# Seven block products in place of eight for the second MLP product, with weight sums on GpSimd and weight chunks prepared two ahead

## The chip, the cores and the metric

The kernel runs on one core of a Trainium2 chip. A core has five engines with a queue each: TensorE (PE, with its weight loads shown as PEld), VectorE (DVE), ScalarE (ACT), GpSimd (POOL) and SyncE (SP, which issues the DMAs here). The metric is the device time of one execution in microseconds; the kernel before takes 947.76 us, the median of three runs (947.66 to 948.29).

## The reference

Two decoder layers on 256 tokens of width 1024, all in float32. Each layer runs three token mixers side by side, gates and sums them, and then a squared-ReLU MLP. Only the MLP's last line is computed in another way by the change:

```python
def hybrid_layer(x, ...):
    hn = rms_norm(x, norm1_g)
    proj = hn @ w_in                       # 1024 -> 8216 columns, three mixers, gates
    ...
    x = x + mixed @ w_out
    h2 = rms_norm(x, norm2_g)
    x = x + jnp.square(jax.nn.relu(h2 @ w_ff1)) @ w_ff2      # 1024 -> 4096 -> 1024
    return x
```

## The kernel before

Every product with weights is a float32 product in three terms. A number is split into a rounded part (`hi`, in the type fp32r) and a rest (`lo`); TensorE adds hi x hi, hi x lo and lo x hi into one PSUM bank. Weights come from memory in chunks of 1 MB (128 partitions x 2048 numbers). `prepare` (L148) loads a chunk into one of three `raw` buffers and `split` (L133) makes its `hi` on ScalarE (L138, two casts of 128x1024) and its `lo` on VectorE (L139, two subtractions of 128x1024), into three buffers each. A table, `ORDER` (L142), lists the chunks in the order of use, and `chunk` (L161) prepares `AHEAD` = 1 chunk beyond the one asked for. A scheduler then places the instructions on the engines' queues; each engine works its queue in order.

The MLP of a layer is the stage that is changed. `ff1(p)` (L758), p = 0 to 15, makes 256 of the 4096 hidden columns: 48 matmuls with 256 moving columns from chunk 42 + p, then the ReLU on VectorE straight from PSUM (L764), the square on ScalarE (L765), and the split of the result, `fh` (L766 on ScalarE, L767 on VectorE). `ff2(p)` (L769) multiplies these 256 hidden columns with 256 rows of the second weight matrix (chunk 58 + p): 2 halves of 128 hidden columns x 2 halves of 128 tokens x 2 halves of 512 outputs x 3 terms = 24 matmuls with 512 moving columns, added up in four banks `acc` that live through the stage (8 block products of three matmuls for each p). The loop runs `ff2(p)`, `ff1(p + 3)`, `ff2(p + 1)` and so on, so that the hidden columns are three steps ahead. The last four p come from chunks 70 to 73, cut by output half, so that the first half of the output can be finished earlier. The end of a layer is one VectorE instruction for each of the four banks (L804): times `r2`, the inverse mean square, plus `x`; then the next layer's norm, or the store of the output.

Buffers of 128x1024 numbers come from a ring of 14 (`s4`, function `slab`), of 128x512 numbers from a ring of 4 (`s2`, `half`): a new tile takes the oldest place and waits until all readers of that place are done.

Of the kernel before, what the change touches and what calls it, by code (L numbers as in the profile page):

```python
# [18 lines left out]
P = 128  # L19
# [24 lines left out]
def kernel(ctx: ExitStack, tc: tile.TileContext, xT, xtok, gbias, wbig, wsml, aup, cst, prm, out):  # L44
# [223 lines left out]
    for l in range(DEPTH):  # L268
# [500 lines left out]
        def ff2(p):  # L769
            h = hs.pop(p)  # L770
            w = [z.rearrange("p (k c) -> p k c", c=D) for z in chunk(l, 58 + p)]
            for k in range(2):
                for t in range(2):
                    ts = slice(t * P, (t + 1) * P)
                    for n in range(2):
                        rows_mm(acc[t][n], w, k, slice(512 * n, 512 * n + 512), h[:, 0, k, ts], h[:, 1, k, ts],
                                p == 0 and k == 0, False)

        NT = 4
        ff1(0)  # L780
        ff1(1)
        acc = [[Bank(pmx, f"fa{l}{t}{n}", [P, 512]) for n in range(2)] for t in range(2)]
        ff1(2)
        for p in range(16 - NT):
            ff2(p)
# [7 lines left out]
        for n in range(2):
            for a in range(2):
                w = [z.rearrange("p (k c) -> p k c", c=512) for z in chunk(l, 70 + 2 * n + a)]
                for t in range(2):
                    ts = slice(t * P, (t + 1) * P)
                    for k in range(4):
                        h = hs[16 - NT + 2 * a + k // 2]
                        rows_mm(acc[t][n], w, k, slice(0, 512), h[:, 0, k % 2, ts], h[:, 1, k % 2, ts],  # L800
                                False, a == 1 and k == 3)
                    if a == 1:
                        xs = x[:, t, 512 * n:512 * n + 512]
                        nc.vector.scalar_tensor_tensor(xs, acc[t][n].t, r2[:, t:t + 1], xs, op0=OP.mult, op1=OP.add)  # L804
                        if l + 1 < DEPTH:
                            norm.squares(t, n)
                        else:
                            nc.sync.dma_start(out[:, t, 512 * n:512 * n + 512], xs)
# [43 lines left out]
def _pack(w_in, brs, w_out, w1, w2):  # L852
    c = []
    cut = lambda a, n: w_in[:, a:a + n]
    c += _tok(cut(GV, 512)) + _tok(cut(GG, 512)) + _chan(cut(GQ, 512)) + _chan(cut(GK, 512))
# [4 lines left out]
    for w in brs:  # L860
        for h in range(2):
            c.append(w[:, 512 * h:512 * h + 512].reshape(4, P, 512).transpose(1, 0, 2).reshape(P, CHW))
    left, right = _tok(w_out[:, :512]), _tok(w_out[:, 512:])
    c += [left[0], right[0], left[1], right[1]]
    c += _chan(w1)
    for p in range(12):
        c.append(w2[T * p:T * (p + 1)].reshape(2, P, D).transpose(1, 0, 2).reshape(P, CHW))
    c += _tok(w2[12 * T:, :512]) + _tok(w2[12 * T:, 512:])
    return c


# [55 lines left out]
```

## Time and profile before

| | before |
|---|---|
| median of three runs | 947.76 us |
| the profiled execution | 946.03 us |
| its span in the trace | 944.3 us |
| mean granted TensorE clock (1 is 2.4 GHz) | 0.995 |
| PE busy | 918.5 us, 97%, 5188 matmuls |
| DVE busy | 624.0 us, 66% |
| ACT busy | 454.0 us, 48% |
| POOL busy | 65.9 us, 7%, 84 instructions |

The durations in the prediction come from the one profiled execution (946.03 us, 1.7 us below the median of the runs). A row with a line and an engine gives busy time and the mean of one; a timeline row gives start, duration, engine, line and operation. An instruction's duration includes the time in which it stands started and blocked, so the spacing of two neighbours in a full queue tells more than their durations.

### The profile page before, as it was taken

To read this page: it belongs to the slowest core of one execution; us is meant where nothing else is said; L and a number is where in the kernel's file an instruction comes from. 1 tells how busy PE (TensorE), PEld (TensorE's weight loads), DVE (VectorE), ACT (ScalarE), POOL (GpSimd) and SP (SyncE) were. 2 spreads that over 40 slices of the span, in tenths; PEclk is the share of its full clock that TensorE was granted. 3 is DMA by queue.
4 is the path that set the end of the run, shared out by engine and by line. 5 is a ranking of instruction groups with operands and counts; after the bars stand their busy time and mean duration, and the time that the engine had idled before them with its cause. 6 is when DMAs were issued, how large, how long until landed. Compare 5 with 4: busy or idle time off the path is not lost.

```text
span 944.3 us, 12865 instructions
## 1 busy us (share of the span) xinstructions
PE 918.5 (97%) x5188; PEld 789.2 (84%) x5188; DVE 624.0 (66%) x984; ACT 454.0 (48%) x647; POOL 65.9 (7%) x84
## 2 busy tenths in 40 slices
PE   7799999999999999999999999999999999999998
PEld 5578888788788999999887788878887899999996
DVE  5995668477876655555669955765788675555553
ACT  5756444454435544444557553435443454444441
POOL 1551000000110000000002300000002000000000
PEclk9799999999999999999999999999999999999999
DMA  9547343544455555555442554344544545545541
GB/s 333 219 159 262 141 145 110 190 170 154 170 178 178 179 179 189 199 192 179 178 173 106 197 216 145 134 145 178 188 147 166 185 160 203 179 178 185 194 157 45
DMA packets 26203, 164.91 MB, mean 175 GB/s; under 512 B 3040, under 2 KB 3296, under 8 KB 7328
## 3 DMA queue, kind: packets, MB, share of 16 engines
q1 hardware_dynamic: 26144, 164.10, 48.7%
q8 instruction: 40, 0.66, 0.3%
q14 instruction: 19, 0.16, 0.0%
HBM read 163.04 MB, written 1.05 MB: 174 GB/s over the span
## 4 chain that ended last, share of the span: by engine, by line
PE 85%; DVE 10%; issue 2%; ACT 1%; DMA 1%; SPq 0%; POOL 0%; DVEq 0%
PE fa L75 19%; PE bg L75 10%; PE wo L75 5%; DVE lo L139 4%; PE br L75 3%; PE gk L75 3%; PE gq L75 2%; PE lq L75 2%; PE lo L75 2%; PE gg L75 2%; PE lv L75 2%; PE mv L75 2%; PE gv L75 2%; PE mk L75 2%; PE sc L75 1%
## 5 line engine op out<-in xcount | busy, mean ns | idle before, releaser
L138 ACT CAST hi<-raw 128x1024 fp32r<-128x1024 f32 x296 | 301.4, 1047 | 384.9 <-issue 112.0
L139 DVE TENSOR_TENSOR lo<-raw,hi 128x1024 fp32r<-128x1024 f32 x296 | 362.5, 1244 | 139.4 <-ACT hi L138 139.0
L75 PE MATMUL fa<-hi,fh 128*128 128x512 f32 x512 | 162.3, 390 | 0.0
L75 PEld LDWEIGHTS fa<-hi,fh 128*128 128x128 f32 x512 | 96.2, 188 | 19.6
L75 PE MATMUL fa<-lo,fh 128*128 128x512 f32 x256 | 100.0, 391 | 0.0
L75 PE MATMUL bg<-hi,xha 128*128 128x512 f32 x192 | 77.3, 404 | 4.1 <-ACT hi L138 4.1
L75 PE MATMUL bg<-lo,xha 128*128 128x512 f32 x192 | 76.2, 397 | 5.0 <-DVE lo L139 5.0
L75 PE MATMUL bg<-hi,xla 128*128 128x512 f32 x192 | 75.8, 395 | 0.0
L75 PEld LDWEIGHTS fa<-lo,fh 128*128 128x128 f32 x256 | 48.2, 188 | 8.9
L75 PEld LDWEIGHTS bg<-lo,xha 128*128 128x128 f32 x192 | 36.7, 191 | 13.7 <-DVE lo L139 6.5
L75 PEld LDWEIGHTS bg<-hi,xha 128*128 128x128 f32 x192 | 36.6, 191 | 13.0 <-ACT hi L138 4.3
L75 PEld LDWEIGHTS bg<-hi,xla 128*128 128x128 f32 x192 | 36.6, 191 | 7.7
L75 PE MATMUL wo<-hi,mh 128*128 128x512 f32 x64 | 25.7, 401 | 0.0
L75 PE MATMUL wo<-hi,ml 128*128 128x512 f32 x64 | 25.0, 390 | 0.0
L75 PE MATMUL wo<-lo,mh 128*128 128x512 f32 x64 | 25.0, 390 | 0.0
L414 DVE SCALAR_TENSOR_TENSOR gate<-bg,ny,gb 128x512 f32<-128x512 f32 x24 | 17.3, 748 | 9.2 <-PE bg L75 9.2
L767 DVE TENSOR_TENSOR fh<-fs,fh 128x512 fp32r<-128x512 f32 x32 | 21.9, 684 | 0.0
L721 DVE SCALAR_TENSOR_TENSOR gate<-gate,br 128x512 f32<-128x512 f32 x24 | 16.4, 682 | 6.3 <-PE br L75 6.2
L765 ACT ACTIVATE fs<-fs 128x512 f32<-128x512 f32 x32 | 20.1, 628 | 0.1
L766 ACT CAST fh<-fs 128x512 fp32r<-128x512 f32 x32 | 19.7, 616 | 0.0
L75 PE MATMUL lq<-xha,hi 128*128 128x256 f32 x64 | 18.6, 291 | 0.0
L75 PE MATMUL gk<-xha,hi 128*128 128x256 f32 x64 | 18.5, 289 | 0.0
(542 smaller groups left out, 2201.0 us busy)
## 6 DMA issues: line engine op xcount, KB each, us to landing
raw<-in_wbig_dram SPq DMA_DIRECT2D x147, 1024.0 KB, 4.7
gb<-in_gbias_dram SPq DMA_DIRECT2D x12, 256.0 KB, 3.2
xT<-in_xT_dram SPq DMA_DIRECT2D x4, 256.0 KB, 4.8
raw<-in_wbig_dram SPq DMA_DIRECT2D x4, 256.0 KB, 6.1
x<-in_xtok_dram SPq DMA_DIRECT2D x2, 512.0 KB, 8.7
out_dram<-x SPq DMA_DIRECT2D x4, 256.0 KB, 2.0
cs<-in_cst_dram SPq DMA_DIRECT2D x1, 752.0 KB, 10.4
raws<-in_wsml_dram SPq DMA_DIRECT2D x2, 256.0 KB, 4.3
```

The costliest lines, as they stand in the source:

```text
L75: self._chain(nc.tensor.matmul(o, lhsT=lhsT, rhs=rhs, start=start, stop=stop, skip_group_check=True))
L138: nc.scalar.copy(hi[:, sl], raw[:, sl])
L139: nc.vector.tensor_sub(lo[:, sl], raw[:, sl], hi[:, sl])
L414: nc.vector.scalar_tensor_tensor(g[:, t], bs[t].t, r[:, t:t + 1], bias, op0=OP.mult, op1=OP.add)
L721: nc.vector.scalar_tensor_tensor(g[:, t], g[:, t], 1.0, b.t, op0=OP.add, op1=OP.mult)
L765: nc.scalar.activation(s, s, AF.Square)
L766: nc.scalar.copy(h[:, 0], s)
L767: nc.vector.tensor_sub(h[:, 1], s, h[:, 0])
```

## The change

The second MLP product is computed in Strassen's form (Winograd's variant). Tokens, hidden columns and outputs are each cut into two halves (128 tokens, 16 x 128 hidden columns, 512 outputs). In place of eight block products of the halves there are seven, each between a sum or difference of hidden blocks and a sum or difference of weight blocks, each in a PSUM bank of its own (four of the pool `pmx`, three of `pmm`).

- The weight chunk p now holds four 512-column blocks: two hidden halves x two output halves. `sums` makes three sums from them on GpSimd before the split: `t` (128x1024), one block written over a block of `raw` (128x512), and `t4` (128x512). Besides `hi` and `lo` of the chunk it makes the split of `t` (`th`, `tl`) and of `t4` (`t4h`, `t4l`).
- `ff1(p)` puts the ReLU on ScalarE, makes three sums of hidden blocks on VectorE (128x256, 128x128, 128x128) and splits eight blocks (128x1024) in place of four.
- `ff2` makes 7 x 3 = 21 matmuls of 512 columns for each p in place of 24.
- At the end of a layer the seven banks are combined with seven VectorE or ScalarE instructions and four that add to `x`. p = 14 and 15 of all seven products come last.
- `AHEAD` is 2 for all chunks of the kernel, the ring `s2` has 9 places, and the space that is set aside for DMA descriptors is smaller. The weights of both MLP products are laid out in another order in memory.

```diff
-AHEAD = 1
+AHEAD = 2
-    s2 = ctx.enter_context(tc.tile_pool(name="s2", bufs=4))
+    s2 = ctx.enter_context(tc.tile_pool(name="s2", bufs=9))
+    def sums(tag, raw):
+        b = raw.rearrange("p (i c) -> p i c", c=512)
+        t, t4 = slab(f"t{tag}", shape=(P, 2, 512)), half(f"t4{tag}")
+        nc.gpsimd.tensor_add(t, b[:, 0:4:3], b[:, 1:2].to_broadcast([P, 2, 512]))
+        nc.gpsimd.tensor_add(b[:, 1], t[:, 0], b[:, 3])
+        nc.gpsimd.tensor_add(t4, b[:, 1], b[:, 2])
+        hi, lo = split(tag, raw, CHW)
+        th, tl = slab(f"th{tag}", F32R, (P, 2, 512)), slab(f"tl{tag}", F32R, (P, 2, 512))
+        t4h, t4l = half(f"t4h{tag}", F32R), half(f"t4l{tag}", F32R)
+        for r, h, o in ((t, th, tl), (t4, t4h, t4l)):
+            nc.scalar.copy(h, r)
+            nc.vector.tensor_sub(o, r, h)
...
-    ORDER += [42, 43, 44] + [j for p in range(13) for j in (58 + p, 45 + p)][:-2] + [57, 70, 71, 72, 73]
+    ORDER += [42, 43, 44] + [j for p in range(13) for j in (58 + p, 45 + p)] + [71, 72, 73]
...
-        ready[l, j] = split(f"{l}_{j}", raw, CHW)
+        ready[l, j] = sums(f"{l}_{j}", raw) if j >= 58 else split(f"{l}_{j}", raw, CHW)
...
+        SIDES = {"P1": (0, "11"), "Q6": (6, "T2"), "P7": (4, "T3"), "Q4": (3, "T4"), "P2": (2, "21"), "P5": (5, "T1"),
+                 "P3": (7, "22")}
...
-            nc.vector.tensor_scalar(s, b.t, 0.0, None, op0=OP.max)
-            nc.scalar.activation(s, s, AF.Square)
-            nc.scalar.copy(h[:, 0], s)
-            nc.vector.tensor_sub(h[:, 1], s, h[:, 0])
+            nc.scalar.activation(s, b.t, AF.Relu)
+            nc.scalar.activation(q[:, 0:4], s, AF.Square)
+            nc.vector.tensor_sub(q[:, 4:6], q[:, 0:4:3], q[:, 1:2].to_broadcast([P, 2, P]))
+            nc.vector.tensor_add(q[:, 6], q[:, 0], q[:, 5])
+            nc.vector.tensor_sub(q[:, 7], q[:, 6], q[:, 2])
+            h = hs[p] = [slab(f"fh{p}", F32R, shape=(P, 8, P)), slab(f"fl{p}", F32R, shape=(P, 8, P))]
+            nc.scalar.copy(h[0], q)
+            nc.vector.tensor_sub(h[1], q, h[0])
+        def ff2(name, p, w):
+            i, side = SIDES[name]
+            b, (hh, hl), (wh, wl) = acc[name], hs[p], w
+            b.mm(b.t, hh[:, i], wh[side], p == 0, False)
+            b.mm(b.t, hh[:, i], wl[side], False, False)
+            b.mm(b.t, hl[:, i], wh[side], False, p == 15)
...
+        for p in range(14):
+            w = chunk(l, 58 + p)
+            for name in SIDES:
+                ff2(name, p, w)
             if p + 3 < 16:
                 ff1(p + 3)
...
+        for name in SIDES:
+            for p in (14, 15):
+                ff2(name, p, w[p - 14])
+            z = acc[name].t
+            if name == "P1":
+                nc.scalar.copy(p1, z)
...
+            else:
+                nc.vector.tensor_add(cv_, z, cv_)
+                put(0, 1, cv_, nr2)
```

In the changed program the order of the queues is as follows at three places of the first layer. VectorE, one step of the MLP loop of before (chunk 50 is for `ff1(8)`, chunk 64 for `ff2(6)`; `fs` and `fh` belong to `ff1`):

```order
L139 TENSOR_TENSOR lo_50_3194<-raw_50_3191,hi_50_3193 128x1024 x2
L764 TENSOR_SCALAR fs_3186<-f_7__3136 128x512
L139 TENSOR_TENSOR lo_64_3226<-raw_64_3223,hi_64_3225 128x1024 x2
L767 TENSOR_TENSOR fh_3185<-fs_3186,fh_3185 128x512
L139 TENSOR_TENSOR lo_51_3289<-raw_51_3286,hi_51_3288 128x1024 x2
```

The same step now (`fq` and `fl` belong to `ff1(7)`, `tl` and `t4l` to the sums of chunk 64):

```order
L139 TENSOR_TENSOR lo_50_3240<-raw_50_3237,hi_50_3239 128x1024 x2
L139 TENSOR_TENSOR lo_64_3313<-raw_64_3305,hi_64_3312 128x1024
L787 TENSOR_TENSOR fq_3295<-fq_3295 128x256
L788 TENSOR_TENSOR fq_3295<-fq_3295 128x128
L789 TENSOR_TENSOR fq_3295<-fq_3295 128x128
L792 TENSOR_TENSOR fl_3302<-fq_3295,fh_3301 128x1024
L155 TENSOR_TENSOR tl_64_3319<-t_64_3307,th_64_3318 128x1024
L139 TENSOR_TENSOR lo_64_3313<-raw_64_3305,hi_64_3312 128x1024
L155 TENSOR_TENSOR t4l_64_3321<-t_64_3308,t4h_64_3320 128x512
L139 TENSOR_TENSOR lo_51_3350<-raw_51_3347,hi_51_3349 128x1024 x2
```

A step of VectorE grows from six instructions, of which five have both inputs in SBUF, to eleven, all with both inputs in SBUF. The half of chunk 64 that holds the rewritten block is split after `tl`, as the last but one of the step.

GpSimd, from the last work of the first layer's mixers on, of before:

```order
L610 TENSOR_SCALAR ly<-ly 128x4
L723 TENSOR_TENSOR gate_1181<-gate_1181,gate_422 128x512 x2
L723 TENSOR_TENSOR gate_1580<-gate_1580,gate_616 128x512 x2
L322 TENSOR_SCALAR hr<-ny 128x2
L352 TENSOR_TENSOR mkro<-mku,tabs_4185 128x512
```

Two steps of the MLP loop now, in which `t` first waits for VectorE and for TensorE, the readers of the ring place that it takes:

```order
L147 TENSOR_TENSOR t_63_3197<-raw_63_3195 128x1024 [waits DMAHW7_49,DVE_49,PE_49]
L148 TENSOR_TENSOR raw_63_3195<-t_63_3197,raw_63_3195 128x512 [waits DMAHW4_49,DVE_49,Pool_49]
L149 TENSOR_TENSOR t_63_3198<-raw_63_3195 128x512 [waits Pool_49]
L147 TENSOR_TENSOR t_64_3307<-raw_64_3305 128x1024 [waits DMAHW1_49,DVE_49,PE_49]
L148 TENSOR_TENSOR raw_64_3305<-t_64_3307,raw_64_3305 128x512 [waits DMAHW6_49,DVE_49,Pool_49]
L149 TENSOR_TENSOR t_64_3308<-raw_64_3305 128x512 [waits Pool_49]
```

GpSimd had nothing between the mixers and the next layer (`gate`, then `hr`); now 16 x 3 sums stand there for each layer.

TensorE, the end of the first layer's MLP now, from the first use of the rewritten half of the last chunk's `lo` on (`fa0P`, `fa0Q` are banks of the seven products):

```order
L75 MATMUL fa0P_2748<-lo_73_4206,fh_4194 128x512
L75 MATMUL fa0P_2748<-hi_73_4205,fl_4195 128x512
L75 MATMUL fa0Q_2749<-lo_73_4206,fh_4194 128x512
L75 MATMUL fa0Q_2749<-hi_73_4205,fl_4195 128x512
L75 MATMUL fa0Q_2751<-t4l_73_4214,fh_4194 128x512
L75 MATMUL fa0Q_2751<-t4h_73_4213,fl_4195 128x512
L75 MATMUL fa0P_2754<-hi_72_4124,fh_4071 128x512
L75 MATMUL fa0P_2754<-lo_72_4125,fh_4071 128x512
L75 MATMUL fa0P_2754<-hi_72_4124,fl_4072 128x512
L75 MATMUL fa0P_2754<-hi_73_4205,fh_4194 128x512
L75 MATMUL fa0P_2754<-lo_73_4206,fh_4194 128x512
L75 MATMUL fa0P_2754<-hi_73_4205,fl_4195 128x512
```

Of before, the last six matmuls stood at the same place in one bank:

```order
L75 MATMUL fa_2652<-hi_73_4012,fh_3913 128x512
L75 MATMUL fa_2652<-lo_73_4013,fh_3913 128x512
L75 MATMUL fa_2652<-hi_73_4012,fh_3913 128x512 x2
L75 MATMUL fa_2652<-lo_73_4013,fh_3913 128x512
L75 MATMUL fa_2652<-hi_73_4012,fh_3913 128x512
```

The matmuls of the last two chunks are mixed now, so that twelve are left when the last halves are split.

## Rows read from the trace of the kernel before

**Rows 1.** The profile page, busy time (us), share of the span, instructions.
```profile
PE 918.5 (97%) x5188; PEld 789.2 (84%) x5188; DVE 624.0 (66%) x984; ACT 454.0 (48%) x647; POOL 65.9 (7%) x84
```

**Rows 2.** Chain of waits, first layer's MLP: start us, us, engine, tile, line, instructions.
```profile
299.16 3.00 PE f__2526 L75 x25
...
343.62 5.75 PE f__2946 L75 x48
349.37 5.47 PE fa L75 x24
...
468.86 10.01 PE fa L75 x44
```

**Rows 3.** Windows: one loop step; both MLP stages. Busy us and (instructions) per engine, clock.
```profile
338.15:349.37 11.22, 11.22 (x74) 10.26 (x73) 6.11 (x6) 5.04 (x7) 0.00 (x0) 1.00 0.55 191
...
299.20:478.90 179.70, 179.70 (x1157) 164.13 (x1155) 102.00 (x110) 84.17 (x111) 0.00 (x0) 1.00 0.50 178
761.70:940.50 178.80, 178.76 (x1147) 163.15 (x1145) 96.82 (x102) 77.57 (x97) 0.00 (x0) 1.00 0.46 165
```

**Rows 4.** Groups of VectorE and ScalarE in 315.7 to 450.3 us: busy us, mean ns.
```profile
L139 DVE TENSOR_TENSOR lo<-raw,hi 128x1024 fp32r<-128x1024 f32 x48 | 57.8, 1224 | 33.6 <-ACT hi L138 33.6
...
L138 ACT CAST hi<-raw 128x1024 fp32r<-128x1024 f32 x49 | 50.1, 1046 | 76.8 <-PE fa L75 30.5 <-PE f__2851 L75 3.6 <-PE f__3326 L75 3.6
```

**Rows 5.** Timeline of GpSimd, 57 to 73 us: start us, us, operation.
```profile
57.23 3.22 POOL L438 TENSOR_TENSOR az<-az,rTa 128x1024 f32<-128x1024 f32 x1 [14.36 <-ACT az L436]
...
67.27 1.39 POOL L329 TENSOR_TENSOR tabs<-cs,prm 128x64 f32<-128x64 f32 x1
...
72.67 0.32 POOL L329 TENSOR_TENSOR tabs<-cs,prm 128x64 f32<-128x64 f32 x1
```

**Rows 6.** Timeline of VectorE, 56.9 to 67.2 us.
```profile
56.97 1.22 DVE L139 TENSOR_TENSOR lo<-raw,hi 128x1024 fp32r<-128x1024 f32 x1
58.10 2.90 DVE L352 TENSOR_TENSOR mqro<-mqu,tabs 128x512 f32<-128x512 f32 x1
...
66.44 0.68 DVE L358 TENSOR_TENSOR mqro<-mqro,mqtmp 128x512 f32<-128x512 f32 x1
67.05 0.29 DVE L174 SCALAR_TENSOR_TENSOR mqt<-mqy 128x16 f32<-128x16 f32 x1
```

**Rows 7.** Timeline of VectorE and GpSimd, 247 to 252 us.
```profile
247.56 1.13 DVE L614 SCALAR_TENSOR_TENSOR ymls<-nu,ly,lo 128x128 f32<-128x128 f32 x4
...
247.62 1.27 POOL L723 TENSOR_TENSOR gate<-gate,gate 128x512 f32<-128x512 f32 x1
250.04 1.29 POOL L723 TENSOR_TENSOR gate<-gate,gate 128x512 f32<-128x512 f32 x1 [1.14 <-DVE gate L721]
...
250.40 2.01 DVE L139 TENSOR_TENSOR lo<-raw,hi 128x1024 fp32r<-128x1024 f32 x1 [0.44 <-ACT hi L138]
```

**Rows 8.** TensorE after waits: timeline rows, with the idle time before in brackets.
```profile
27.61 0.79 PE L75 MATMUL bg<-hi,xha 128*128 128x512 f32 x1 [4.09 <-ACT hi L138]
...
35.21 0.63 PE L75 MATMUL bg<-hi,xla 128*128 128x512 f32 x1
35.64 0.63 PE L75 MATMUL bg<-hi,xha 128*128 128x512 f32 x1
...
498.58 0.74 PE L75 MATMUL z<-gs,us 96*128 96x256 f32 x4 [2.00 <-DVE gs L379]
```

**Rows 9.** Windows around those waits; the column before the last two is the granted clock.
```profile
33.00:35.00 2.00, 2.00 (x8) 1.71 (x7) 2.00 (x9) 0.24 (x1) 0.00 (x0) 0.50 0.51 147
...
497.00:499.00 2.00, 0.42 (x3) 0.42 (x4) 1.94 (x3) 1.85 (x3) 2.00 (x4) 1.00 0.25 95
```

**Rows 10.** Waits of TensorE for weights: us in total, times, longest us.
```profile
PE bg L75 <- DVE lo L139: 5.0, 3, 2.8
PE bg L75 <- ACT hi L138: 4.1, 1, 4.1
```

**Rows 11.** Timeline of VectorE at the end of the program.
```profile
940.50 0.75 DVE L804 SCALAR_TENSOR_TENSOR x<-fa,nr,x 128x512 f32<-128x512 f32 x1 [1.97 <-PE fa L75]
```

More of the change, by code (lines that the diff above doesn't have):

```diff
@@ L140, in split @@
         return hi, lo
+    def sums(tag, raw):
[10 more added lines that the diff above has]
+            nc.vector.tensor_sub(o, r, h)
+        hi, lo = (a.rearrange("p (i c) -> p i c", c=512) for a in (hi, lo))
+        side = lambda m, u, u4: {"11": m[:, 0], "T2": m[:, 1], "21": m[:, 2], "22": m[:, 3], "T1": u[:, 0],
+                                 "T3": u[:, 1], "T4": u4}
+        return side(hi, th, t4h), side(lo, tl, t4l)
     ORDER = ["s", 10, 11, 20, 21, 8, 9, 22, 23, 12, 13, 0, 1, 4, 5, 6, 7, 24, 25, 14, 15, 16, 17, 26, 27, 2, 3, 18, 19]
     ORDER += [28, 29, 30, 31, 32, 34, 36, 33, 35, 37, 38, 39, 40, 41]
-    ORDER += [42, 43, 44] + [j for p in range(13) for j in (58 + p, 45 + p)][:-2] + [57, 70, 71, 72, 73]
+    ORDER += [42, 43, 44] + [j for p in range(13) for j in (58 + p, 45 + p)] + [71, 72, 73]
     ORDER = [(l, j) for l in range(DEPTH) for j in ORDER]
@@ L755 @@
         hs = {}
-        acc = []
+        acc = {}
+        SIDES = {"P1": (0, "11"), "Q6": (6, "T2"), "P7": (4, "T3"), "Q4": (3, "T4"), "P2": (2, "21"), "P5": (5, "T1"),
+                 "P3": (7, "22")}
         def ff1(p):
@@ L761, in ff1 @@
                 norm.inverse()
-            h = hs[p] = slab(f"fh{p}", F32R, shape=(P, 2, 2, T))
-            s = half(f"fs{p}", shape=(P, 2, T))
-            nc.vector.tensor_scalar(s, b.t, 0.0, None, op0=OP.max)
-            nc.scalar.activation(s, s, AF.Square)
-            nc.scalar.copy(h[:, 0], s)
-            nc.vector.tensor_sub(h[:, 1], s, h[:, 0])
[L769 to L785, printed above, removed]
+            s = half(f"fs{p}", shape=(P, 4, P))
+            q = slab(f"fq{p}", shape=(P, 8, P))
+            nc.scalar.activation(s, b.t, AF.Relu)
+            nc.scalar.activation(q[:, 0:4], s, AF.Square)
+            nc.vector.tensor_sub(q[:, 4:6], q[:, 0:4:3], q[:, 1:2].to_broadcast([P, 2, P]))
@@ L786 @@
+        for p in range(3):
+            ff1(p)
+        for i, name in enumerate(SIDES):
+            acc[name] = Bank(pmx if i < 4 else pmm, f"fa{l}{name}", [P, 512])
+        for p in range(14):
+            w = chunk(l, 58 + p)
+            for name in SIDES:
+                ff2(name, p, w)
             if p + 3 < 16:
                 ff1(p + 3)
-        for p in range(16 - NT + 3, 16):
-            ff1(p)
+        w = [chunk(l, 72), chunk(l, 73)]
         r2 = norm.r2
+        nr2 = small("nnr2", [P, 2])
@@ L791 @@
+        nc.gpsimd.tensor_scalar(nr2, r2, -1.0, None, op0=OP.mult)
         if l + 1 < DEPTH:
             norm = Norm(f"a{l + 1}", prm_t[l + 1][:, Q_G1:Q_G1 + 8])
[L793 to L808, printed above, removed]
-            if l + 1 < DEPTH:
-                norm.turn(n)
+        add, sub = OP.add, OP.subtract
@@ new lines, in put @@
+        def put(t, n, v, f):
+            xs = x[:, t, 512 * n:512 * n + 512]
+            nc.vector.scalar_tensor_tensor(xs, v, f[:, t:t + 1], xs, op0=OP.mult, op1=OP.add)
+            if l + 1 < DEPTH:
+                norm.squares(t, n)
+            else:
+                nc.sync.dma_start(out[:, t, 512 * n:512 * n + 512], xs)
+        p1, cw_, c21, cv_, u = (half(f"ev{i}") for i in range(5))
+        for name in SIDES:
[4 more added lines that the diff above has]
+                nc.scalar.copy(p1, z)
+            elif name == "Q6":
+                nc.vector.tensor_sub(cw_, z, p1)
+            elif name == "P7":
+                nc.vector.tensor_sub(c21, z, cw_)
+            elif name == "Q4":
+                nc.vector.tensor_add(u, z, c21)
+                put(1, 0, u, r2)
+            elif name == "P2":
+                nc.vector.tensor_add(p1, z, p1)
+                put(0, 0, p1, r2)
+                if l + 1 < DEPTH:
+                    norm.turn(0)
+            elif name == "P5":
+                nc.vector.tensor_add(c21, z, c21)
+                put(1, 1, c21, nr2)
+                nc.vector.tensor_sub(cv_, z, cw_)
+            else:
+                nc.vector.tensor_add(cv_, z, cv_)
+                put(0, 1, cv_, nr2)
+                if l + 1 < DEPTH:
+                    norm.turn(1)
@@ L864, in _pack @@
     c += [left[0], right[0], left[1], right[1]]
[L865 to L868, printed above, removed]
+    c += _chan(w1.reshape(D, 2, 16, P).transpose(0, 2, 1, 3).reshape(D, 4 * D))
+    c += list(w2.reshape(2, 16, P, D).transpose(1, 2, 0, 3).reshape(16, P, CHW))
     return c
```

2 lines of the change are left out of this document (1 added, 1 removed).

## The prediction

> **What bounds the kernel now.** I read the page first: TensorE is busy in 97% of the span, GpSimd in 7% [rows 1]. Then the chain of waits, to see whether TensorE really sets the time in the stage that changes. It does: the chain runs through nothing but matmuls there, 5.75 us for an `ff1` and 5.47 us for an `ff2`, in turn, without a gap [rows 2]. A step (one of each) is 11.22 us, of which VectorE works 6.11 us, ScalarE 5.04 us and GpSimd nothing [rows 3]. The stage is 179.7 us in the first layer and 178.8 us in the second [rows 3], and both end with the last matmul. So fewer matmuls shorten the time as long as the other engines still finish a step in what TensorE then needs. The last thing I read are timelines of places where VectorE and GpSimd work at once, since the change puts both to work in every step; of before they never do in this stage.
>
> **What is removed.** `ff2` goes from 24 to 21 matmuls. A matmul costs 5.47 / 24 = 0.228 us [rows 2], so an `ff2` falls to 4.79 us and a step to 10.54 us; 16 x 2 x 3 x 0.228 = 21.9 us for both layers, if TensorE stays the bound.
>
> **What is added, engine by engine, for a step.** ScalarE had 5.04 us and gets two casts more (`th` 1.05 as a cast of 128x1024 [rows 4], `t4h` about 0.6), the ReLU (about 0.6), and a split of 1024 in place of 512 (+0.4): about 7.7 us. It fits.
>
> VectorE, by the spacing of neighbours in a full queue. A two-input instruction over 1024 takes 58.10 - 56.97 = 1.13 us [rows 6], over 512 67.05 - 66.44 = 0.61 us [rows 6]; four over 128 take 1.13 us, 0.28 us each [rows 7]; for 256 I take 0.39 us, an estimate on the line between the last two. A step has four `lo` (4.52), `tl` (1.13), `t4l` (0.61), the three sums `fq` (0.39 + 0.28 + 0.28) and `fl` (1.13): 8.34 us.
>
> GpSimd: 1.28 us for a sum over 512 [rows 7]. The one over 1024 is shown once, at 3.22 us [rows 5], but it starts at 57.23 us while a VectorE `lo` runs until 58.10 us [rows 6]; without those 0.87 us it is 2.35 us. I take 2.30 us: twice 1.28 us less one start-up of about 0.26 us (a product over 64 takes 0.32 us [rows 5]) comes to that. Three sums: 4.86 us.
>
> Each engine alone fits into 10.54 us. Together they don't, and this is the step on which the forecast rests. In every place of the trace where a GpSimd sum and a VectorE instruction with both inputs in SBUF overlap, one stands until the other is done. The VectorE product `mqro` over 512 starts at 58.10 us behind the GpSimd product that runs from 57.23 to 60.45 us and takes 2.90 us in place of 0.68 us [rows 5, 6]: it ends 0.55 us after that one does. A `lo` that starts at 250.40 us inside a GpSimd sum (250.04 to 251.33 us) takes 2.01 us [rows 7]: the 0.93 us that are left of the sum, and 1.1 us of its own. The other way round, GpSimd's 0.32 us product takes 1.39 us behind a `lo` [rows 5]. The one kind that isn't held is `ymls`, which has one tensor input in PSUM [rows 7]. All of the 8.34 us on VectorE are of the held kind; the ReLU from PSUM, which was not, has left it.
>
> The Trainium skill speaks against this change at the same point: its page "SBUF — State Buffer", section "Who interferes with whom", says that GpSimd and VectorE share a pair of ports, and that a VectorE instruction with two SBUF inputs and a GpSimd instruction that reads SBUF block one another for the whole of the instruction, whichever started first. The trace agrees (2.90 us against 0.68 us). By that rule a step is the sum of both engines, without it TensorE's 10.54 us.
>
> So a step needs 8.34 + 4.86 = 13.20 us of VectorE and GpSimd in turn, more than TensorE's 10.54 us and than the 11.22 us of before. I laid one step out by hand in the queue order shown, E being the end of an `ff2`, from which `t` may start (it takes the ring place of that `ff2`'s hidden columns): `t` until E + 2.4, the last `fq` until 2.7, the second sum until 4.1, `fl` 5.2, `t4` 6.5, `tl` 7.6, the rewritten half of `lo` 8.8, `t4l` 9.4, the two `lo` for `ff1` 11.6, the other half of `lo` 12.8, then the next `fq`. `ff1` ends at E + 5.75, and the second matmul of `ff2` needs the `lo` of 8.8; 20 x 0.228 us later, at E + 13.4, comes the next E. The hands-over cost about 0.2 us. What is late next is therefore not the weights' DMA but the splits, and TensorE waits some 3 us in each step.
>
> **The sum for a layer.** Work that can't overlap, from the stage's start at 299.2 us: GpSimd 16 x 4.86 = 77.8; `lo` of the second product's chunks 32 x 1.13 = 36.2; `tl` 18.1; `t4l` 9.8; `fq` and `fl` 16 x 2.08 = 33.3; `lo` of the `ff1` chunks that are not yet split then, 14 x 2.26 = 31.6. Together 206.8 us. The first chunk's sums (4.9) can run ahead, in the stage before, where GpSimd is free: 201.9. Hands-over 14 x 0.2 = 2.8. After the last split twelve matmuls stand, 2.7 us. That gives 207.4 us in place of 179.7 and 178.8: +27.7 and +28.6.
>
> The ends: in the second layer one VectorE instruction over 512 stands between the last matmul and the one that was last (0.75 us [rows 11]), +0.7; in the first layer the longer combination is partly covered by the next layer's first matmuls, which need only half of the columns: +1.0. Preparing two chunks ahead elsewhere: TensorE waits 9.1 us for splits in the gates' products [rows 10], at places where VectorE is full (2.00 of 2.00 us [rows 9]), so that an earlier request finds no free VectorE; and in the start one more chunk of 1 MB stands in SP's queue ahead of `x` and the constants. I put the two at nothing, with -9 and +9 as ends.
>
> Sum: 27.7 + 28.6 + 0.7 + 1.0 = 58. The profiled execution takes 946.0 us, 1.7 us below the median, so 946.0 + 58 + 1.7 = **1006 us**.
>
> Ends of the unknown parts: if an instruction holds the other engine only for 95% of its spacing, -10 us a layer; if a hand-over costs 1 us a step and not 0.2, +11 us a layer. With the ends of the preparation that is 977 to 1037 us.
>
> **Rivals.**
> *TensorE stays the bound.* The three sums use strided and repeated operands, and the overlaps shown are single pairs, not a steady stream; if VectorE and GpSimd could work side by side here, a step would be 10.54 us, and the ring place that `t` waits for would not hinder: 2.3 + 1.28 + 1.05 + 1.13 + 4.56 = 10.3 us from E to the next E. Time: 947.8 - 21.9 + 1.7 = 928 us. Against it: no pair in the trace overlaps freely when both VectorE inputs are in SBUF. If GpSimd were held for its own time only in half of the cases, a step would be near 11.2 us and the time near 948 us.
>
> *The clock falls in the gaps.* After TensorE stood 4.09 us at 23.5 to 27.6 us (and 2.81 us more soon after) it ran at 0.50, the lower level of 1.2 GHz, with matmuls of 512 columns 0.43 us apart [rows 8, 9]; a gap of 2.00 us left it at 1.00 [rows 8, 9]. My gap of 3 us, in two parts, lies between. At the lower level an `ff1` takes 5.75 x 0.43 / 0.228 = 10.8 us, 2 us past the split for which it would wait anyway, and an `ff2` 9.0 us, 4.2 us more, after which TensorE has no gap and gets its clock back. If that happens in every second step, it is 14 x 2 x 6.2 / 2 = 87 us on top at most, half of it if only one of the two parts falls: 1050 to 1093 us. The Trainium skill describes such a swing under "HAM oscillation — how this bites in real kernels" on the page "TensorE: Matmul & The Clock Gate": waits in a loop that throttle the array again and again. No stage of this trace shows it repeat; the one fall at 27 us agrees.
>
> *The preparation two ahead pays by itself.* If the mixers gained all of the 9.1 us, the forecast would still be 997 us; it decides nothing.
>
> **How the numbers follow.** Forecast with its ends (977 to 1037): 0.70. Clock swing (1037 to 1093): 0.14. TensorE bound (922 to 946): 0.10. Half-held (946 to 977): 0.06, of which 0.02 within 0.2% of before, which is about what a measurement of this kernel can tell from no change. Faster 0.10, same 0.02, slower 0.88. The range of 8 in 10 takes the forecast's ends and a part of the two neighbours: 970 to 1050 us.
>
> **What would show it.** Right: in the first layer's stage the steps are 13 to 14 us apart; VectorE's groups `lo` and `fl` have means well above 1.22 us and GpSimd's over 512 above 1.28 us, since each holds waits for the other; TensorE waits in `ff2` for `lo` of L139, some 3 us a step, and GpSimd's and VectorE's own work together fill the step. Wrong: steps of 10.5 us with unchanged means (no holding), or matmuls of 512 columns 0.43 us apart in the stage (clock), or stages that are unchanged while the mixers moved.

## The result and the profile after

The changed kernel takes 1045.48 us, the median of four runs (1045.34 to 1046.31), against 947.76 us: a ratio of 1.1032 with a 95% interval of 1.1012 to 1.1051. That is 97.7 us slower; +58 was forecast (1006 us, 970 to 1050), so the direction and the kind of loss were as forecast and its size was 40 us short. The profiled execution has a span of 1043.6 us, 99.3 more than before.

The page's busy times of the kernel after, to be held against [rows 1]:

```profile
PE 938.4 (90%) x5092; PEld 790.8 (76%) x5092; DVE 837.4 (80%) x1126; ACT 529.3 (51%) x745; POOL 273.7 (26%) x182
```

TensorE has 96 matmuls less and is no longer busy throughout; that its busy time is 20 us longer all the same goes with its lower mean granted clock, 0.959 for 0.995. VectorE is up by 213 us and GpSimd by 208 us, far more than the instructions alone would take, because each one's busy time now holds waits for the other.

The two MLP stages, from the first `ff1` matmul to the last of the second product (columns as in [rows 3]):

```profile
296.84:521.50 224.66, 190.08 (x1113) 165.23 (x1111) 200.77 (x169) 118.57 (x152) 104.59 (x49) 0.92 0.40 144
810.50:1035.05 224.55, 187.46 (x1113) 163.72 (x1111) 199.51 (x167) 116.85 (x149) 105.45 (x49) 0.93 0.37 131
```

Between the same matmuls the stages of before take 181.4 us (297.47 to 478.86) and 180.4 us (760.04 to 940.47). So the 99.3 us are: first stage +43.3, second stage +44.1, from the first stage's last matmul to the second stage's first +7.8, after the last matmul +4.7 (3.8 before, 8.6 after), and -0.6 before the first stage.

Two steps in the middle of the first stage, in the same columns:

```profile
373.50:387.54 14.04, 11.19 (x69) 9.60 (x69) 12.80 (x12) 7.34 (x10) 6.82 (x4) 1.00 0.41 151
387.54:401.58 14.04, 12.21 (x68) 10.54 (x68) 12.80 (x12) 7.34 (x11) 6.73 (x4) 0.88 0.43 149
```

Each of the two steps is 14.04 us long, against 11.22 [rows 3], and VectorE is busy for 12.80 of them. One step's VectorE and GpSimd, as timelines (start us, us, engine, line, operation, tiles):

```profile
393.72 0.41 DVE L787 TENSOR_TENSOR fq<-fq 128x256 f32<-128x256 f32 x1
...
394.50 0.29 DVE L789 TENSOR_TENSOR fq<-fq 128x128 f32<-128x128 f32 x1
395.96 1.23 DVE L792 TENSOR_TENSOR fl<-fq,fh 128x1024 fp32r<-128x1024 f32 x1 [1.17 <-ACT fh L791]
397.10 1.22 DVE L155 TENSOR_TENSOR tl<-t,th 128x1024 fp32r<-128x1024 f32 x1
398.24 3.42 DVE L139 TENSOR_TENSOR lo<-raw,hi 128x1024 fp32r<-128x1024 f32 x1
401.57 1.78 DVE L155 TENSOR_TENSOR t4l<-t,t4h 128x512 fp32r<-128x512 f32 x1
```

```profile
388.84 1.61 POOL L149 TENSOR_TENSOR t<-raw 128x512 f32<-128x512 f32 x1
397.60 2.97 POOL L147 TENSOR_TENSOR t<-raw 128x1024 f32<-128x1024 f32 x1 [7.16 <-DMA raw<-in_wbig_dram]
400.65 2.16 POOL L148 TENSOR_TENSOR raw<-t,raw 128x512 f32<-128x512 f32 x1
```

Two things are to be seen. The `lo` at 398.24 us takes 3.42 us where it took 1.22 [rows 6]: GpSimd's `t` runs from 397.60 to 400.57 us, and `lo` ends 1.1 us after it. `t4l` (1.78 us for 0.68) stands behind the second sum in the same way. And at 394.8 us, when the last `fq` is done, VectorE stands for 1.17 us until ScalarE has cast `fh`, while GpSimd stands too, since its next chunk has not landed. Neither works in that gap, and it is there in 14 steps of each layer.

The groups of VectorE and GpSimd in 330 to 460 us (busy us, mean ns, idle before and its releaser), to be held against [rows 4]:

```profile
L139 DVE TENSOR_TENSOR lo<-raw,hi 128x1024 fp32r<-128x1024 f32 x38 | 75.3, 2018 | 0.0
...
L148 POOL TENSOR_TENSOR raw<-t,raw 128x512 f32<-128x512 f32 x10 | 21.5, 2153 | 0.8
L149 POOL TENSOR_TENSOR t<-raw 128x512 f32<-128x512 f32 x10 | 16.7, 1666 | 0.8
L155 DVE TENSOR_TENSOR t4l<-t,t4h 128x512 fp32r<-128x512 f32 x10 | 16.6, 1663 | 0.0
...
L792 DVE TENSOR_TENSOR fl<-fq,fh 128x1024 fp32r<-128x1024 f32 x9 | 11.0, 1226 | 10.5 <-ACT fh L791 10.5
```

The mean `lo` is 2018 ns for 1224. What TensorE waits for (us in total, times, longest us):

```profile
PE fa0P L75 <- DVE lo L139: 28.1, 13, 3.3
PE fa1P L75 <- DVE lo L139: 26.0, 12, 3.2
PE fa1P L75 <- ACT hi L138: 7.9, 4, 5.3
...
PE nta L78 <- DVE x L822: 4.2, 1, 4.2
```

The first two lines are `ff2`'s wait for `lo`, 25 times in the 28 steps, as the prediction said it would look. The last line is the first layer's end, where the next norm waits for the combined output `x`.

### The profile page after: what moved, and what is told of

Same layout as the page of the kernel before. It is cut to its first block, busy times and chain, and to the rows that moved or that the text cites. A ratio compares the mean times of both kernels' runs of the same rounds, so it can differ in the third digit from the quotient of the medians.

```text
span 1043.6 us, 13089 instructions
## 1 busy us (share of the span) xinstructions
PE 938.4 (90%) x5092; PEld 790.8 (76%) x5092; DVE 837.4 (80%) x1126; ACT 529.3 (51%) x745; POOL 273.7 (26%) x182
## 3 DMA queue, kind: packets, MB, share of 16 engines
HBM read 163.04 MB, written 1.05 MB: 157 GB/s over the span
## 4 chain that ended last, share of the span: by engine, by line
PE 50%; DVE 34%; issue 9%; ACT 6%; DMA 1%; SPq 0%; DVEq 0%; POOL 0%; ACTq 0%
DVE lo L139 16%; PE bg L75 9%; PE wo L75 4%; DVE t4l L155 3%; DVE fl L792 3%; PE br L75 3%; ACT fh L791 2%; PE gk L75 2%; PE gq L75 2%; PE lq L75 2%; DVE tl L155 2%; PE lo L75 2%; PE gg L75 2%; PE mk L75 2%; PE lv L75 2%
## 5 line engine op out<-in xcount | busy, mean ns | idle before, releaser
L139 DVE TENSOR_TENSOR lo<-raw,hi 128x1024 fp32r<-128x1024 f32 x296 | 443.6, 1525 | 63.4 <-ACT hi L138 62.9
L147 POOL TENSOR_TENSOR t<-raw 128x1024 f32<-128x1024 f32 x32 | 91.8, 2868 | 193.5 <-DMA raw<-in_wbig_dram 156.4
L791 ACT CAST fh<-fq 128x1024 fp32r<-128x1024 f32 x32 | 33.5, 1048 | 195.7 <-DVE fq L789 195.7
L792 DVE TENSOR_TENSOR fl<-fq,fh 128x1024 fp32r<-128x1024 f32 x32 | 41.1, 1285 | 37.4 <-ACT fh L791 37.4
L148 POOL TENSOR_TENSOR raw<-t,raw 128x512 f32<-128x512 f32 x32 | 64.3, 2009 | 2.5
L149 POOL TENSOR_TENSOR t<-raw 128x512 f32<-128x512 f32 x32 | 53.7, 1678 | 2.5
L155 DVE TENSOR_TENSOR t4l<-t,t4h 128x512 fp32r<-128x512 f32 x32 | 50.2, 1569 | 0.0
L75 PE MATMUL fa0P<-lo,fh 128*128 128x512 f32 x48 | 22.2, 463 | 28.1 <-DVE lo L139 28.1
L75 PEld LDWEIGHTS bg<-lo,xha 128*128 128x128 f32 x192 | 36.7, 191 | 13.2 <-DVE lo L139 6.0
L155 DVE TENSOR_TENSOR tl<-t,th 128x1024 fp32r<-128x1024 f32 x32 | 41.2, 1286 | 0.0
L75 PEld LDWEIGHTS fa0P<-lo,fh 128*128 128x128 f32 x48 | 10.0, 208 | 34.5 <-DVE lo L139 32.8
L154 ACT CAST th<-t 128x1024 fp32r<-128x1024 f32 x32 | 33.4, 1045 | 0.0
## 6 DMA issues: line engine op xcount, KB each, us to landing
x<-in_xtok_dram SPq DMA_DIRECT2D x2, 512.0 KB, 10.7
```

Source lines behind the costliest of these rows:

```text
L75: self._chain(nc.tensor.matmul(o, lhsT=lhsT, rhs=rhs, start=start, stop=stop, skip_group_check=True))
L147: nc.gpsimd.tensor_add(t, b[:, 0:4:3], b[:, 1:2].to_broadcast([P, 2, 512]))
L148: nc.gpsimd.tensor_add(b[:, 1], t[:, 0], b[:, 3])
L149: nc.gpsimd.tensor_add(t4, b[:, 1], b[:, 2])
L154: nc.scalar.copy(h, r)
L155: nc.vector.tensor_sub(o, r, h)
```

## The experiments

The theory at this point (A): VectorE's and GpSimd's work on SBUF excludes each other; a step is the sum of the two, 12.8 us, and a gap of 1.2 us in which neither works. The rivals: (B) the step is a loop of waits through the raw ring, the transfer and ScalarE, whatever GpSimd does; (C) TensorE's lower clock; and, for the 40 us that were not forecast, the preparation two ahead.

**The sums left out.** The splits read raw blocks in place of the sums.

```diff
-        t, t4 = slab(f"t{tag}", shape=(P, 2, 512)), half(f"t4{tag}")
-        nc.gpsimd.tensor_add(t, b[:, 0:4:3], b[:, 1:2].to_broadcast([P, 2, 512]))
-        nc.gpsimd.tensor_add(b[:, 1], t[:, 0], b[:, 3])
-        nc.gpsimd.tensor_add(t4, b[:, 1], b[:, 2])
+        t, t4 = b[:, 0:4:3], b[:, 2]
```

> The changed kernel without the three GpSimd sums of each second-product chunk: the splits that read the sums read raw blocks of the same shapes instead, so VectorE, ScalarE and TensorE keep every instruction and only GpSimd's work of 4.86 us a step is left out (the weight sums are the part of the computation that is missing). Theory A (VectorE and GpSimd exclude each other on SBUF, so their 8.3 and 4.9 us add up in a step of 14.03 us): VectorE's own 8.3 us fit under TensorE's 10.5 to 11.2, the step falls to 10.5 to 11.3 us, the mean of the lo instructions comes back to about 1.2 us, and the time to 930 to 962 us (before's 947.8, less up to 18 for the matmuls saved, plus 6 to 13 for the combinations at the layer's ends). Rival B (the step is a chain of waits, raw ring and ScalarE's cast of the hidden blocks, whatever GpSimd does): the step stays above 13 us, time above 1015. Rival C (TensorE at the lower clock costs the time): granted clock and step unchanged, 1030 to 1050.

Measured: 928.79 us, 116.7 less than the changed kernel, ratio to before 0.981 (0.9791 to 0.9829). A step, in the columns of the windows above:

```profile
373.30:383.84 10.54, 10.54 (x71) 9.70 (x70) 8.52 (x10) 7.42 (x10) 0.00 (x0) 1.00 0.52 197
```

It is TensorE's 10.54 us to the last digit, with VectorE down from 12.80 to 8.52 us busy by the same instructions. Rivals B and C fall: TensorE has no wait left in the step, and the granted clock (0.993 over the run) came back with the work; it followed the gaps and did not make them. `AHEAD`, the ring of nine, the order of the weights and the smaller descriptor space are those of the changed kernel here, so none of them makes the loss by itself. But this run takes away more than the hold. In its VectorE queue a `lo` (373.43 us) stands directly before `fl` (374.57 us), so the 1.17 us gap is gone as well, and `t` takes no place in a ring; the 116.7 us are the price of all of it together, and the runs below take it apart. The time is just under the range given: 947.8 less 21.9 for the matmuls is 925.9, so all that the change adds at the ends costs about 3 us net here, where TensorE sets the pace, and not the 6 to 13 that I set down for the combinations.

**The sums on VectorE.** `nc.gpsimd` becomes `nc.vector` in the three sums.

> The same three sums moved from GpSimd to VectorE; the whole computation is there. VectorE does a 128x1024 float32 subtraction in 1.13 us and a 128x512 one in 0.61, so the sums are about 2.35 us there against 4.86 on GpSimd. Theory A: the step is VectorE's 8.3 + 2.35 = 10.7 us, up to 1.2 more if its wait for ScalarE's cast stays: 10.7 to 11.9 against TensorE's 10.5 to 11.2. Stages of 16 steps, two layers: 930 to 985 us, most likely 960, and so 60 to 115 us under the changed kernel. Rival B (chain of waits): the sums become one more link on VectorE, 1030 to 1060 us.

Measured: 997.07 us, ratio 1.0516 (1.0495 to 1.0537): the same additions, 48.4 us faster, on the engine that was already the bound. The step is 12.13 us, somewhat above the range given (10.7 to 11.9), and the time is 12 us above its range (930 to 985, most likely 960). The gap of the changed kernel stands unchanged in it:

```profile
L792 DVE TENSOR_TENSOR fl<-fq,fh 128x1024 fp32r<-128x1024 f32 x11 | 13.5, 1226 | 12.9 <-ACT fh L791 12.9
...
L147 DVE TENSOR_TENSOR t<-raw 128x1024 f32<-128x1024 f32 x10 | 12.2, 1218 | 0.0
```

`t` takes 1.22 us here, and on GpSimd 2.41 us alone (302.83 us in the changed kernel, shown further down) and 2.9 us with its waits. 12.9 / 11 = 1.17 us a step go to the wait for `fh`.

**One chunk ahead again.** `AHEAD = 1` in the changed kernel.

> The changed kernel with chunks prepared one ahead again. Theory A: the step is the sum of VectorE's and GpSimd's own work, which doesn't depend on how early it is done: within 9 us of 1045.5 where the stage is concerned. Rival (two ahead hides the 4.8 us of the raw transfer and the chain sum, split, cast): without it they stand in every step, 3 to 5 us x 28 steps, 1130 to 1190 us. The opposite rival (two ahead blocks the raw ring and takes the ring's places from the next chunk): 1010 to 1030.

Measured: 1046.62 us, a ratio to before of 1.1045 (1.1028 to 1.1062); steps of 13.9 to 14.1 us. And the counterpart, **the kernel before with `AHEAD = 2`**:

> The kernel before with its weight chunks prepared two ahead instead of one, nothing else. Theory: the raw ring of three and the split ring of three set how far ahead the work can be, so the stages that TensorE sets don't change: 940 to 953. Rival (the earlier splits hold the ring's places and delay the chunk that is wanted next, which would then be part of the changed kernel's loss): above 957.

Measured: 946.13 us, ratio 0.9978 (0.9968 to 0.9988). So preparing two ahead gives before 1.6 us, just measurable, and gives the changed kernel nothing that can be told; it has no part in the loss.

**Three sums in the kernel before**, in `prepare`, into tiles that nobody reads:

```diff
+        if 58 <= j < 74:
...
+            nc.gpsimd.tensor_add(t, b[:, 0:4:3], b[:, 1:2].to_broadcast([P, 2, 512]))
+            nc.gpsimd.tensor_add(t4, t[:, 0], b[:, 3])
+            nc.gpsimd.tensor_add(t4, b[:, 1], b[:, 2])
```

> The kernel before with three GpSimd sums of the same shapes added to each of the 16 second-product chunks of a layer, into tiles that nothing reads. Theory A: VectorE's share of a step there is about 5.1 us, so 5.1 + 4.9 = 10 us still fits under the step's 11.22 us that TensorE sets: VectorE's lo instructions become longer by 0.5 to 2 us each, and the time stays within 10 us of 947.8. Rival (GpSimd's sums slow TensorE, the transfers or the chunk's ring by themselves): each step longer by 1 us or more, above 975 us.

Measured: 955.90 us, +8.3, ratio 1.0089 (1.0073 to 1.0104).

```profile
L139 DVE TENSOR_TENSOR lo<-raw,hi 128x1024 fp32r<-128x1024 f32 x46 | 74.8, 1648 | 24.7 <-ACT hi L138 24.7
```

`lo` is held as in the changed kernel (1648 ns on the mean), and yet the steps after the first few are 11.22 us as before: VectorE had room for it there. The loss comes where the stages begin and end. In the two traces, which are 10.5 us apart, 4.7 us come before the first layer's first square on ScalarE (306.07 us before, 310.77 here), nothing from there to its last (456.98 and 461.69), 2.8 from there to the last `fa` matmul (478.47 and 485.98), 1.8 more up to the second layer's first square (768.82 and 778.17), 0.2 from there to its last, and 1.0 behind it. At the entry a held `lo` (296.68 us, 3.27 us long) makes the residual sum `x` late, at the end held instructions make `fh` and `x` late, and TensorE waits for them:

```profile
301.38 0.44 PE L78 MATMUL ntb<-cs,x 128*128 128x128 f32 x2 [1.70 <-DVE x L755]
...
469.23 0.73 PE L75 MATMUL fa<-hi,fh 128*128 128x512 f32 x2 [1.14 <-DVE fh L773]
...
474.36 0.33 PE L78 MATMUL nta<-cs,x 128*128 128x128 f32 x1 [1.20 <-DVE x L810]
```

So the hold alone does not make a kernel slower; a hold on an engine without slack does.

**The gap filled.** ScalarE casts `th` ahead of `fh`, and VectorE does `tl` (and a `lo`) ahead of `fl`; the sums stay on GpSimd. `late` keeps `fh` and `fl` back until the next chunk's sums are split:

```diff
-            nc.scalar.copy(h[0], q)
-            nc.vector.tensor_sub(h[1], q, h[0])
+            late.append((h, q))
...
-            nc.scalar.copy(h, r)
-            nc.vector.tensor_sub(o, r, h)
+            flush(nc.scalar.copy(h, r), nc.vector.tensor_sub(o, r, h))
```

> The changed kernel (sums on GpSimd) with ScalarE's th ahead of fh and VectorE's fl behind tl, so that VectorE has tl and a lo to do in the 1.17 us in which it waited for fh. Theory A (in the step of 14.03 us, 12.8 are VectorE's and GpSimd's work one after the other and 1.2 are that wait): step 12.8 to 13.2 us, time 1010 to 1025. Rival B (GpSimd's t waits for the raw transfer, which starts when VectorE's last lo gives a place of the raw ring back, so the loop through raw ring, transfer, sums and splits sets the step and the wait for fh lies inside it): step 13.8 to 14.1, time 1038 to 1048.

Measured: 1012.49 us, 33.0 less than the changed kernel, ratio 1.0681 (1.0665 to 1.0697).

```profile
390.33:403.11 12.78, 11.15 (x72) 9.63 (x71) 12.71 (x11) 7.63 (x9) 6.57 (x3) 1.00 0.46 164
```

The step is 12.78 us and VectorE's queue has no gap left, at a granted clock of 1.00 in this step. 2 x 14 x 1.17 = 32.8 us is what theory A gives for the gaps. That the total agrees so closely is in part chance: 24.6 us of it come between the first and the last matmul of the two stages, and the rest between and behind them. GpSimd still waits 6.05 us for a raw chunk, and that wait costs nothing while VectorE is full. This run, and not the one without sums, rules out the form of rival B in which the chain from the raw ring through transfer and sums to the splits sets the step.

**Four places for raw chunks** (`wraw` with 4 in place of 3, `s2` with 8 in place of 9).

> The changed kernel with four places for raw chunks instead of three (and eight instead of nine for the half tiles, to make room). Theory A: the transfer then lands before VectorE's wait for fh, GpSimd's sums can use that time, and GpSimd's 7.16 us wait for the transfer goes: step 12.8 to 13.4 us, time 1010 to 1030. Rival B (the sums start earlier but meet VectorE's instructions in another place, the exclusive sum plus the wait for fh stays): step 13.9 to 14.1, time 1040 to 1048.

Measured: 1029.11 us, ratio 1.0857 (1.0841 to 1.0873). The wait for `fh` is still there, but now GpSimd works in it, and most steps are 12.8 to 13.2 us:

```profile
378.47:391.46 12.99, 10.83 (x71) 9.60 (x70) 11.75 (x10) 7.32 (x9) 6.80 (x4) 1.00 0.44 162
```

So the gap was dead time for both engines for two reasons at once: VectorE waited for the cast and GpSimd for a place in the ring. Taking away either one shortens the step, this one less evenly (two steps are still 13.9 and 14.1 us) and for only half of the gain, 16.4 us against 33.0. The place less for half tiles was not tried by itself.

**One sum of the three on VectorE** (`t`; the other two stay on GpSimd).

> Only the first of the three sums (t, 128x1024) is moved to VectorE; the two of 128x512 stay on GpSimd. Theory A (each sum costs the step its own length on whichever of the two engines does it): t costs VectorE 1.2 us where GpSimd took 2.3, the other two 1.28 each where VectorE takes 0.65, so the step lies between the 12.13 us of all on VectorE and the 14.03 of all on GpSimd, at 12.9 to 13.4, time 1015 to 1032. Rival (one instruction of GpSimd in the loop is enough to break VectorE's pace, by the hand-over and the chain t, sum, t4 across two engines): 13.9 or more, 1040 to 1060.

Measured: 1033.62 us, ratio 1.0906 (1.0888 to 1.0924). The step is 13.39 us, within the range, and the time 1.6 us above it. A wait had come in that I had not expected, VectorE's `tl` for ScalarE's `th`, 1.11 us a step, because `t` is now made just before its cast:

```profile
382.42 1.38 DVE L155 TENSOR_TENSOR tl<-t,th 128x1024 fp32r<-128x1024 f32 x1 [1.11 <-ACT th L154]
```

In sum: no sum on GpSimd 12.13 us, two 13.39 (1.11 of it that wait), three 14.04.

**The sums on VectorE with the gap filled**: `fl` behind the next chunk's `t`.

> The sums on VectorE as in the run before, and fl (VectorE's subtraction that waits for ScalarE's cast fh) is put behind t, the next chunk's first sum, on VectorE's queue. In the run before, every step was 12.13 us: VectorE busy 10.96 us and 1.17 us of waiting for fh. Theory: the wait is filled by t (1.2 us), the step is 10.9 to 11.1 us, and over the 13 or 14 such steps of each layer 30 to 33 us go: 962 to 970. Rival (the wait moves to another VectorE instruction, such as tl behind th): the step stays above 11.8 us, 985 to 998.

Measured: 955.89 us, ratio 1.0085 (1.0070 to 1.0100), better than expected: the step is 10.75 us, since the gap went and VectorE works at the spacing of a full queue throughout.

```profile
388.96:399.71 10.75, 10.75 (x72) 9.77 (x71) 10.68 (x14) 7.53 (x10) 0.00 (x0) 1.00 0.56 199
```

**And three more edits**: seven hidden blocks in `fh` and `fl`, since one of the eight is no operand of any product; the first chunk's sums before the first hidden pair; the next layer's first `lo` behind the combination.

```diff
-            nc.scalar.copy(h[0], q)
-            late.append((h[1], q, h[0]))
+            nc.scalar.copy(h[0][:, 0:7], q[:, 0:7])
+            late.append((h[1][:, 0:7], q[:, 0:7], h[0][:, 0:7]))
...
+                prepare(*ORDER[done[0]])
+                done[0] += 1
...
+            if hold and tag in ("1_10", "1_11"):
+                after(i, hold[-1])
```

> The run with the sums on VectorE and fl behind t, with three more edits: fh and fl over the seven hidden blocks that the products use instead of eight (128x896 instead of 128x1024, some 0.13 us of VectorE a step), chunk 58's sums in the 3 us in which VectorE stands idle before the first hidden pair of a layer is done, and the next layer's first two weight chunks split after the combinations of the second product instead of among them (four lo, 4.7 us, once). Theory: TensorE and VectorE are both within 0.2 us of a step of 10.54 to 10.65 us; 4 us go from the loops, 4 to 5 from the two layers' starts and 3 to 5 from the layer's end: 955.9 less 11 to 14, 941 to 946, under the kernel before. Rival (VectorE's total work in a stage is what counts, so that what is moved ahead or behind is paid elsewhere): only the 4 us of the smaller fh and fl go, 950 to 953.

Measured: 941.87 us, ratio to before 0.9933 (0.9919 to 0.9946): 5.9 us faster than the kernel before and 103.6 faster than the changed one.

```profile
384.34:394.84 10.50, 10.50 (x71) 9.66 (x71) 10.47 (x14) 7.54 (x10) 0.00 (x0) 1.00 0.57 202
```

TensorE is without a gap here and VectorE has 0.03 us of slack. 13 us are left to the run without sums. In the first layer 1.1 of them are there when the stage starts (297.7 us for 296.6), 1.8 more when it ends (469.4 for 466.5), and 5.0 more when the next layer's `mq` products start (508.4 for 500.5): the end, where VectorE is late with the combinations, is the dearest part. The run is faster than the kernel before for both reasons together: from 10.75 to 10.50 us a step is 7 us in 28 steps, and the other half of the 14.0 us that the last three edits win lies outside the steady steps.

## Why the prediction was right, and where it was short

**In part by luck.** The price given to the mechanism was 1006 us with ends of 977 and 1037, and 1045.5 us lies outside these ends. It lies inside the 970 to 1050 us only because that range took in a part of the clock rival's band (1037 to 1093 us), a rival that cost nothing in the steps (below).

**The mechanism held.** The step on which the forecast rests is that VectorE and GpSimd stand while the other works. The run without sums shows it (12.80 us of VectorE become 8.52 with the same instructions), and so do the sums on VectorE. What this part costs was forecast as 8.34 + 4.86 = 13.20 us; with the gap filled it is 12.78, 0.4 us less. VectorE's own part is 8.52, so GpSimd's three sums add 4.3 us and not 4.86; why they add less than their own length alone was not tested. The rule of the Trainium skill ("SBUF — State Buffer", section "Who interferes with whom"), that a VectorE instruction with two SBUF inputs and a GpSimd instruction that reads SBUF block one another, agrees with this trace: 12.78 us is near the 8.52 + 4.86 = 13.38 us of the two, and far from TensorE's 10.54.

Of the signs set down, the steps, the means of `lo` (2018 ns) and of GpSimd's sums over 512 (2153 and 1666 ns), and TensorE's waits came. `fl` was not held in the steady steps (1226 ns), since GpSimd stands when it runs, and the two engines' work does not fill the step. One sign of being wrong came too, matmuls of 512 columns 0.43 us apart, and was harmless (below). "The one kind that isn't held" was too narrow a reading of the trace of before: the reduction `mqss` (L342, one input) keeps its 0.68 us at 62.36 us inside a GpSimd product that runs from 62.11 to 63.04 us. Nothing in the forecast rests on it.

**The term that failed: "The hands-over cost about 0.2 us".** I had laid a step out by hand with `t` at its start, behind the last `ff2`, and `fl` right behind the second sum, as if it were ready. In the trace `t` is made nearly a step early and starts when its raw chunk lands; the cast `fh` can't begin before the last `fq`; and nothing stands between the last `fq` and `fl` in VectorE's queue that could go first. The hand-over is 1.17 us in each of 14 steps of a layer, 16.4 us in place of 2.8: for both layers 27 of the 40 us. I had put 1 us a step at the upper end (+11 us a layer), and the measured value lies beyond that. The rows for it were there to be counted: a cast of 128x1024 takes 1.05 us on ScalarE [rows 4], VectorE's queue order has `fl` directly behind `fq`, and a cast between two neighbours of one queue is a bubble of its own length unless something else stands between.

**The stage.** From 299.2 us I forecast 207.4 us: 201.9 of work that excludes, 2.8 of hands-over and 2.7 behind the last split. It took 222.3 (to 521.50 us). In 204.4 of these one of the two engines is busy, and in 17.9 neither is, 16.4 of them the 14 gaps of 1.17. So of the missing 14.9 us the gaps are 13.6, the work 2.5 more than forecast, and the rest 1.2 less. The 2.5 are a balance that was not taken apart: the steady steps are 0.4 us shorter each, and the first chunk's sums (302.83 to 308.85 us), which I had put ahead of the stage, fell into it, beside instructions of the norm and the combinations that the sum had left out. GpSimd was idle ahead of the stage, but the first instruction in its queue was the sign change `nnr`, which waits for the norm:

```profile
302.64 0.22 POOL L814 TENSOR_SCALAR nnr<-nr 128x2 f32<-128x2 f32 x1 [33.36 <-DVE nr L239]
302.83 2.41 POOL L147 TENSOR_TENSOR t<-raw 128x1024 f32<-128x1024 f32 x1
```

Whether the sums would have started earlier without it was not tried.

**The ends.** I forecast +0.7 and +1.0 and got +4.7 and +7.8. I had counted what stands behind the last matmul if each bank were combined when it is full. But the seven banks fill within the last steps of a stage in which VectorE is late, so that all combinations stand at the end, eleven of them on VectorE after the last split (eight instructions combine the banks, one on ScalarE and seven on VectorE, not seven in all as said of the change; four add to `x`):

```profile
1031.22 0.68 DVE L155 TENSOR_TENSOR t4l<-t,t4h 128x512 fp32r<-128x512 f32 x1
1033.44 0.69 DVE L836 TENSOR_TENSOR ev<-fa1Q,ev 128x512 f32<-128x512 f32 x1 [1.54 <-ACT ev L834]
...
1039.87 0.75 DVE L822 SCALAR_TENSOR_TENSOR x<-ev,nnr,x 128x512 f32<-128x512 f32 x1
```

In the first layer the next layer's `lo` stand among them as well:

```profile
521.22 0.68 DVE L843 TENSOR_TENSOR ev<-fa0P,ev 128x512 f32<-128x512 f32 x1
521.94 2.36 DVE L139 TENSOR_TENSOR lo<-raw,hi 128x1024 fp32r<-128x1024 f32 x2
524.22 0.68 DVE L840 TENSOR_TENSOR ev<-fa0Q,ev 128x512 f32<-128x512 f32 x1
```

**The rivals.** "TensorE stays the bound", 928 us, did not come, but its price was right: the run without the sums takes 928.8. "Half-held" was priced near 11.2 us a step, though 8.34 and half of 4.86 make 10.8; it did not come. The clock did fall, to 0.88 in some steps and 0.92 over the stage. In the step of 0.88 shown above TensorE ran at the lower level, 1.2 GHz, for some 3 us after it had waited for `lo`:

```profile
387.67 0.50 PE L75 MATMUL fa0P<-lo,fh 128*128 128x512 f32 x1 [2.84 <-DVE lo L139]
...
389.71 0.63 PE L75 MATMUL fa0Q<-t4l,fh 128*128 128x512 f32 x1
390.14 0.63 PE L75 MATMUL fa0Q<-t4h,fl 128*128 128x512 f32 x1
```

It cost the steps nothing: a step is 14.04 us at 1.00 and at 0.88 alike, since TensorE still waits 1.8 us in a step at the lower mean clock (2.8 us at 1.00). The swing that the Trainium skill describes ("TensorE: Matmul & The Clock Gate", section "HAM oscillation — how this bites in real kernels") is there in this trace, without a price in these steps. The preparation two ahead was put at nothing, and in the changed kernel nothing of it can be told.

## What to carry to other kernels

Before work is given to an idle engine, look in the trace for two instructions of that engine and the busy one that overlap: if one stands for the other, and the busy one has no slack, add the times and don't take the larger. Then write down the queue order of the engine that becomes the bound and look for neighbours with another engine's instruction between them; each such pair is a gap in every step, and here it was worth 33 us for a change of order alone. A saving of matmuls has to be paid by the engine that prepares their operands: here 0.7 us a step of TensorE was bought with 4.4 us of VectorE (6.11 before, 10.47 in the last version), and it paid only when VectorE's whole step had come down to TensorE's 10.5 and part of its work at the stages' ends had been moved.

## What was not expected of the hardware

The two engines take turns one instruction at a time. A GpSimd sum of 128x512 that takes 1.28 us alone [rows 7] takes 2.15 us as the mean of the second sum in the steady stage of the changed kernel, and on VectorE each of the instructions beside it is held in turn. With four raw places, where three of each meet, they alternate strictly:

```profile
379.56 2.38 DVE L792 TENSOR_TENSOR fl<-fq,fh 128x1024 fp32r<-128x1024 f32 x1 [1.17 <-ACT fh L791]
381.86 2.32 DVE L155 TENSOR_TENSOR tl<-t,th 128x1024 fp32r<-128x1024 f32 x1
384.09 2.28 DVE L139 TENSOR_TENSOR lo<-raw,hi 128x1024 fp32r<-128x1024 f32 x1
```

```profile
378.43 2.41 POOL L147 TENSOR_TENSOR t<-raw 128x1024 f32<-128x1024 f32 x1 [6.13 <-DVE fq L789]
380.92 2.17 POOL L148 TENSOR_TENSOR raw<-t,raw 128x512 f32<-128x512 f32 x1
383.16 2.13 POOL L149 TENSOR_TENSOR t<-raw 128x512 f32<-128x512 f32 x1
```

Each VectorE instruction of 1.22 us is 2.3 us here, its own length and about one GpSimd sum of 128x512, and each such sum is 2.15 us, its own 1.28 and most of a VectorE instruction. ScalarE's casts beside both are not held: `hi` takes 1042 ns on the mean in 330 to 460 us of the changed kernel, and 1046 before [rows 4].
